# Pooling mixer: moving sums on VectorE, means by constants, dt's small steps in other banks, wide norms by Ln and Exp

## The chip, the core and the metric

The kernel runs on one core of a Trainium2 chip. The metric is the device time of one launch in microseconds (us). Of the core's engines five matter: TensorE (PE in the rows; PEld is its weight load), VectorE (DVE), ScalarE (ACT), GpSimd (POOL) and SyncE (SP), which issues most of the DMA transfers. Each engine works through its own instructions in the order in which they stand, and waits on semaphores for the others. TensorE's clock has two levels, 1.2 and 2.4 GHz; the rows give the granted one as a share of 2.4 GHz (PEclk).

## What is computed

Two layers of a backbone over 512 latent tokens and 256 context tokens. In a layer one wide projection feeds a bidirectional state-space mixer (conv, dt, scan) and a pooling mixer; the two are merged by gates, and a SwiGLU sub-layer follows. The modulation vectors (adaLN) come from a small product of a condition with large weights. The last layer needs no pooling of the context.

```python
# sizes: D_MODEL 1024, SEQ 512 (8 rows of 64), CTX_LEN 256, DEPTH 2, POOL_WIDTH 1024
POOL_WINDOWS = (2, 4, 8, 16)

def rmsnorm(x, g):
    xf = x.astype(jnp.float32)
    y = xf * lax.rsqrt(jnp.mean(xf * xf, axis=-1, keepdims=True) + EPS)
    return (y * g).astype(x.dtype)

def pool_minus_self(u):
    L = u.shape[-2]
    ...
    for gi, k in enumerate(POOL_WINDOWS):
        lo = jnp.clip(t - k // 2, 0, L)
        hi = jnp.clip(t + k // 2, 0, L)
        seg = cs[..., gi * POOL_GROUP:(gi + 1) * POOL_GROUP]
        s = jnp.take(seg, hi, axis=-2) - jnp.take(seg, lo, axis=-2)
        outs.append(s / (hi - lo).astype(jnp.float32)[:, None])
    mean = jnp.concatenate(outs, axis=-1)
    return (mean - uf).astype(u.dtype)

# a layer, for latent and context alike
h = modulate(rmsnorm(x, g_mix[l]), sh1, sc1)
proj = h @ w_in            # z, xbc (conv, then SSD), dt, u_pool, gate logits
dt = softplus(dt_raw + dt_bias)
pm = pool_minus_self(u_pool)          # latent: along each row of 64; context: along 256
pm = einsum('blgi,gio->blgo', pm by 4 groups, pool_w)
o_pool = (pm * pool_scale) @ w_pool_out
x = x + ga1 * ((g_ssd * o_ssd + g_pool * o_pool) @ w_out)
x = x + ga2 * swiglu(modulate(rmsnorm(x, g_ffn[l]), sh2, sc2), ...)
```

## The kernel before

Activations stand as 128 channels on the partitions by tokens in the free dimension: 768 columns in layer 0 (512 latent, 256 context), 512 in layer 1's pooling. A matmul in f32 is done as three in fp32r (lines 199 to 201): operands are split in a high part (a cast on ScalarE, whi at L176 for weights, L524 for activations) and a low part (a subtraction on VectorE, wlo at L178, L525). An *item* is one 128-row tile of a product; `K.run` issues items one after the other, and their results go to eight PSUM banks in rotation: pl (2), ptr (2), pc, pst, and py (2), where py is not in the items' rotation. Weights are fetched by SyncE into three raw buffers (L173).

`pool_path` is the part of a layer in which pooling is done. It runs, in this order:

- eight u items, the pooling input. ScalarE copies each result into one of two padded tiles pu, in which a row of 64 tokens has eight zeros on both sides. Then `fin` makes the moving sum: VectorE adds neighbours (L568), GpSimd adds shifted sums for windows 4, 8 and 16 (L573, none to three adds, twelve a layer), VectorE multiplies by rc, a table of 1/count (L576, context L580), subtracts pu (L578, L581) and the result pm is split (L524, L525) into pq.
- the dt item, evicted by ScalarE to dtraw (L625).
- eight pw items (the grouped product, two pooled tiles each; evicted at L600 and split) and eight po items (the output product, evicted at L611). A pw item asks for two of the pooled tiles; the last two items ask for the eighth.

Beside the items run *side generators*, one step each whenever matmuls worth 2150 ns have been issued (`K.tick`). `dt_gen` turns dtraw into decay factors: transposes (copied by VectorE at L658), a chain of small VectorE operations (L660 to L671, with a polynomial at L666), cumulative sums by matmuls (L679 to L689), and rows written back to memory (L708 transposes, L711 the low part sw on VectorE, then DMAs of arow, erow and jrow; Ln at L731). `ada_vec` makes modulation vectors: it loads 128x512 pieces of adaLN weights into tiles aw and multiplies and sums each on VectorE (L396): 64 products of 32 pieces in layer 0, 32 of 32 in layer 1. `K.drain` ends both before the conv part begins.

`Rms.fin` ends a norm: a matmul with ones sums the squares, then for wide norms (1024 channels) ScalarE's Sqrt (L440) and VectorE's reciprocal (L442), for narrow ones (256) Ln and Exp on ScalarE.

The order of instructions on each engine is made by a tile scheduler that simulates engines; `high_priority` moves an instruction ahead, and `issue_after` keeps it behind a named one.

Of the kernel before, what the change touches and what calls it, by code (L numbers as in the profile page):

```python
# [9 lines left out]
F32 = mybir.dt.float32  # L10
# [6 lines left out]
P = 128  # L17
# [271 lines left out]
def tile_hybrid_ssd_pool_dit(ctx, tc, xin, cond, condr, wada, wadt, pk, win, wdt, wso, wpw, wpo, wo, wgu, wdn,  # L289
# [78 lines left out]

    def ada_vec(l, secs, pool, tag, bufs, stile, burst=1):

# [13 lines left out]
        for i, (h, s, k) in enumerate(todo):  # L384
            if (s, k) == (secs[0], 0):
                sb = [stile() for _ in range(nj)]
                for j in range(nj):
                    nc.sync.dma_start(sb[j], srow[j:j + 1, h * 512:(h + 1) * 512].to_broadcast([P, 512]))
            if i + 1 < len(todo):
                load()  # L390
            for j in range(nj):
                if done % burst == 0:
                    yield
                done += 1
                o = ws[i] if j == nj - 1 else K.tile(pool, tag, bufs, [P, 512])
                V.scalar_tensor_tensor(o[:], ws[i][:], 1.0, sb[j], op0=ALU.mult, op1=ALU.mult,  # L396
                                       accum_out=acc[:, secs.index(s), h, k, j:j + 1])
            if h == 1 and k == KT - 1:
                m = mods[l][:, s]
                V.tensor_tensor(m[:, :, :nj], acc[:, secs.index(s), 0], acc[:, secs.index(s), 1], op=ALU.add)  # L400
                ada_fin(l, s, m, [m[:, q::2, :nj] for q in range(2)], nj)

    class Rms:
# [6 lines left out]
        def add(self, t):  # L410
            c0, c1 = self.c0, self.c1
            q = K.tile(self.pool, "tmp" if self.w == CW else "u", self.tb, [P, self.w])
            A.activation(q[:, c0:c1], t[:, self.off + c0:self.off + c1], AF.Square)
            self.q = q
            if self.acc is None:
                self.acc = q
            else:
                self.eng.tensor_tensor(self.acc[:, c0:c1], self.acc[:, c0:c1], q[:, c0:c1], op=ALU.add)

        def fin(self, m):  # L420
# [3 lines left out]
            if m == 1024:  # L424
                warm = K.tile(cst, "warm", 1, [P, 1])
                A.activation(warm[:], self.q[:, c0:c0 + 1], AF.Sqrt)
            eps = epst if m == 1024 else epsg
            for a in range(c0, c1, 512):
# [4 lines left out]
                else:  # L433
# [5 lines left out]
                    T.matmul(o, oner[:], al, start=False, stop=True)  # L439
                A.activation(r[:, a:b], o, AF.Sqrt if m == 1024 else AF.Ln, bias=eps[:], scale=1.0 / m)  # L440
            if m == 1024:
                V.reciprocal(r[:, c0:c1], r[:, c0:c1])  # L442
            else:
                A.activation(r[:, c0:c1], r[:, c0:c1], AF.Exp, scale=-0.5)

# [77 lines left out]
    def split(t, hi, lo, n):  # L523
        A.copy(hi[:, :n], t[:, :n])  # L524
        V.tensor_tensor(lo[:, :n], t[:, :n], hi[:, :n].bitcast(F32), op=ALU.subtract)  # L525

    def pool_path(l, acts, cx, dp, first, nxt, secs):
# [3 lines left out]
        with K.pool(f"pu{l}", 1) as pup, K.pool(f"pp{l}", 2) as pp, K.pool(f"px{l}", 1) as px:  # L531
# [13 lines left out]
            def u_item(i, r, w=None):  # L545
# [12 lines left out]
                def fin():  # L558
# [7 lines left out]
                    with tc.high_priority() if i < HOT else nullcontext():  # L566
# [3 lines left out]
                        for st in range(1, gi + 1):  # L570
                            sh = 1 << st
                            ln -= sh
                            G.tensor_tensor(s[:, :ln], s[:, :ln], s[:, sh:sh + ln], op=ALU.add)  # L573
                        o = 8 - (1 << gi)
                        r3 = lambda t: t[:, :LAT].rearrange("p (r w) -> p r w", w=64)
                        V.tensor_tensor(r3(pm), s[:, :640].rearrange("p (r w) -> p r w", w=80)[:, :, o:o + 64], r3(rc),  # L576
                                        op=ALU.mult)
                        V.tensor_tensor(r3(pm), r3(pm), ul[:, :, 8:72], op=ALU.subtract)  # L578
                        if cx:
                            V.tensor_tensor(pm[:, LAT:], s[:, 640 + o:640 + o + CTX], rc[:, LAT:], op=ALU.mult)  # L580
                            V.tensor_tensor(pm[:, LAT:], pm[:, LAT:], u[:, 648:904], op=ALU.subtract)  # L581
                        split(pm, *pms[i], n)

# [65 lines left out]
    def dt_gen(l, D, dp):  # L649
# [37 lines left out]
        suf = K.psum("ptr")
        T.matmul(suf[:, :192], mk[:, M_GT:M_GT + P], daf[:, :192], start=True, stop=True)
# [735 lines left out]
```

## Time and profile before

| | us |
|---|---|
| median of 3 runs (2915.68 to 2917.33) | 2916.78 |
| the profiled execution | 2918.18 |
| its span in the profile | 2916.4 |
| busy: TensorE | 2809.3 (96%) |
| busy: VectorE | 2047.1 (70%) |
| busy: ScalarE | 1289.1 (44%) |
| busy: GpSimd | 754.2 (26%) |

Times in the profile are counted from the start of the span. A window shows how long each engine was busy in a stretch; a waits view shows for how long an engine stood in front of an instruction and whose signal ended that; a timeline lists instructions with start, duration and, in brackets, the idle time before them with its releaser. Pooling lies at about 55 to 200 us (layer 0) and 1709 to 1815 us (layer 1).

### The profile page before, as it was taken

What the parts mean: (1) busy time and instruction counts of PE and PEld (TensorE: products, weight loads), DVE (VectorE), ACT (ScalarE), POOL (GpSimd) and SP (SyncE); (2) the same over time, 40 slices, a digit from 0 to 9 for tenths busy, and PEclk for the clock granted to TensorE, in tenths of its full rate; (3) what the DMA queues carried; (4) which work ended last, traced back from release to release, by engine and by line L of the source; (5) the groups of instructions that cost most, each with busy time, mean ns of one, the idle gap of its engine ahead of it and who ended that gap; (6) DMA issues with size and microseconds to landing.
All of it is one profiled execution on the core that took longest, in us unless ns stands there. A gap on an engine that the chain in (4) does not pass through costs nothing.

```text
span 2916.4 us, 43006 instructions
## 1 busy us (share of the span) xinstructions
PE 2809.3 (96%) x16384; PEld 2467.8 (85%) x16384; DVE 2047.1 (70%) x3231; ACT 1289.1 (44%) x2102; POOL 754.2 (26%) x695
## 2 busy tenths in 40 slices
PE   6899999999999999999999988999999989999998
PEld 4688888888889998899999976878888868889998
DVE  6965677777754678856666696677777746877776
ACT  4244544555544124333333454455455542545443
POOL 1300323322221112222222132032322211334443
PEclk8999999999999999999999999999999999999999
DMA  7362222222236754312222365322332248523333
GB/s 262 124 174 86 72 83 90 80 76 80 79 94 203 260 184 134 117 58 78 68 66 73 92 195 151 102 84 94 95 98 87 99 158 310 163 85 98 98 102 119
DMA packets 172847, 347.79 MB, mean 119 GB/s; under 512 B 33312, under 2 KB 74048, under 8 KB 172640
## 3 DMA queue, kind: packets, MB, share of 16 engines
q1 hardware_dynamic: 151872, 314.79, 33.8%
q0 software_dynamic: 12448, 13.20, 1.9%
q10 hardware_dynamic: 8320, 17.05, 1.6%
q8 instruction: 129, 2.11, 0.3%
q14 instruction: 78, 0.64, 0.1%
HBM read 310.20 MB, written 34.74 MB: 118 GB/s over the span
## 4 chain that ended last, share of the span: by engine, by line
PE 83%; DVE 7%; issue 3%; DMA 3%; ACT 2%; POOL 1%; SPq 0%; DVEq 0%; ACTq 0%; POOLq 0%
PE pl L201 11%; PE pl L200 11%; PE pl L199 10%; PE pc L199 4%; PE pc L200 4%; PE pc L201 4%; PE ptr L200 3%; PE ptr L199 3%; PE ptr L201 3%; PE pl L261 3%; PE pl L262 3%; PE pl L263 3%; PE pst L789 2%; PE py L860 2%; PE py L831 2%
## 5 line engine op out<-in xcount | busy, mean ns | idle before, releaser
L199 PE MATMUL pl<-h,whi 128*128 128x512 f32 (+2 forms) x1481 | 565.4, 382 | 6.4 <-ACT whi L176 2.8
L201 PE MATMUL pl<-h,whi 128*128 128x512 f32 (+2 forms) x1481 | 561.9, 379 | 1.8 <-DVE h L466 1.8
L200 PE MATMUL pl<-h,wlo 128*128 128x512 f32 (+2 forms) x1481 | 559.1, 378 | 2.1 <-DVE wlo L178 2.0
L176 ACT CAST whi<-raw 128x1024 fp32r<-128x1024 f32 (+5 forms) x340 | 314.2, 928 | 545.9 <-PE pl L201 167.9
L178 DVE TENSOR_TENSOR wlo<-raw,whi 128x1024 fp32r<-128x1024 f32 (+5 forms) x328 | 374.4, 1144 | 176.4 <-ACT whi L176 168.8
L199 PEld LDWEIGHTS pl<-h,whi 128*128 128x128 f32 x1481 | 279.5, 189 | 55.7 <-issue 8.3
L201 PEld LDWEIGHTS pl<-h,whi 128*128 128x128 f32 x1481 | 279.1, 188 | 52.5 <-issue 7.3
L200 PEld LDWEIGHTS pl<-h,wlo 128*128 128x128 f32 x1481 | 279.4, 189 | 49.9 <-issue 7.3
L199 PE MATMUL pc<-h,whi 128*128 128x256 f32 (+2 forms) x923 | 283.8, 307 | 15.1 <-ACT h L524 12.8
L201 PE MATMUL pc<-h,whi 128*128 128x256 f32 (+2 forms) x923 | 284.1, 308 | 1.7 <-DVE h L459 1.6
L200 PE MATMUL pc<-h,wlo 128*128 128x256 f32 (+2 forms) x923 | 280.0, 303 | 3.1 <-DVE wlo L178 3.1
L1013 DVE SCALAR_TENSOR_TENSOR cv<-up,pk,cv 128x770 f32<-128x770 f32 (+1 forms) x256 | 258.8, 1012 | 21.8 <-ACT cv L1011 15.9
L780 POOL TENSOR_TENSOR sct<-cs,dec 128x256 f32<-128x256 f32 x128 | 125.1, 982 | 441.8 <-ACT cs L791 270.3
L199 PEld LDWEIGHTS pc<-h,whi 128*128 128x128 f32 x923 | 176.3, 191 | 30.0 <-ACT h L524 13.3
L200 PEld LDWEIGHTS pc<-h,wlo 128*128 128x128 f32 x923 | 176.5, 191 | 13.3 <-DVE wlo L178 3.5
L201 PEld LDWEIGHTS pc<-h,whi 128*128 128x128 f32 x923 | 176.3, 191 | 11.9 <-issue 3.8
L200 PE MATMUL ptr<-h,wlo 128*128 128x384 f32 (+3 forms) x493 | 170.4, 346 | 2.9 <-DVE wlo L178 2.8
L199 PE MATMUL ptr<-h,whi 128*128 128x384 f32 (+3 forms) x493 | 170.5, 346 | 1.3 <-ACT whi L176 1.1
L201 PE MATMUL ptr<-h,whi 128*128 128x384 f32 (+3 forms) x493 | 169.4, 344 | 0.0
L863 POOL TENSOR_TENSOR y<-y,ea 128x512 f32<-128x512 f32 x64 | 91.0, 1422 | 243.5 <-DVE ea L862 231.8
L117 POOL TENSOR_TENSOR ss<-raw 128x512 f32<-128x512 f32 x37 | 54.3, 1467 | 342.6 <-DMA raw<-in_wgu 269.7
L105 DVE TENSOR_TENSOR wlo<-raw,whi 128x1024 fp32r<-128x1024 f32 x74 | 111.2, 1502 | 16.4 <-ACT whi L104 16.2
(358 smaller groups left out, 6695.3 us busy)
## 6 DMA issues: line engine op xcount, KB each, us to landing
raw<-in_win SPq DMA_DIRECT2D x144, 512.0 KB, 3.4
raw<-in_wgu SPq DMA_DIRECT2D x92, 512.0 KB, 3.3
aw<-in_wadt SPq DMA_DIRECT2D x64, 256.0 KB, 3.7
ea<-erow SPq DMA_DIRECT2D x128, 128.0 KB, 3.1
raw<-in_wso SPq DMA_DIRECT2D x32, 512.0 KB, 4.7
ss<-in_wadt SPq DMA_DIRECT2D x64, 256.0 KB, 4.0
raw<-in_wo SPq DMA_DIRECT2D x26, 512.0 KB, 3.7
raw<-in_wdn SPq DMA_DIRECT2D x48, 192.0 KB, 2.4
```

Source lines behind the costliest of these rows:

```text
L105: k.nc.vector.tensor_tensor(l, t, h.bitcast(F32), op=ALU.subtract)
L176: nc.scalar.copy(hi[:, :n], raw[:, :n])
L178: e.tensor_tensor(lo[:, :n], raw[:, :n], hi[:, :n].bitcast(F32), op=ALU.subtract)
L199: T.matmul(o, wh, ah[:, c0:c1], start=first, stop=False)
L200: T.matmul(o, wl, ah[:, c0:c1], start=False, stop=False)
L201: T.matmul(o, wh, al[:, c0:c1], start=False, stop=last)
L261: nc.tensor.matmul(o, wh[:, m], ah, start=bool(first) and k == 0, stop=False, skip_group_check=True)
L262: nc.tensor.matmul(o, wl[:, m], ah, start=False, stop=False, skip_group_check=True)
L263: nc.tensor.matmul(o, wh[:, m], al, start=False, stop=k == len(acts) - 1, skip_group_check=True)
L780: G.tensor_tensor(t[:].rearrange("p (h q) -> p h q", h=4), cs[src][:, d, :].rearrange("p (h q) -> p h q", h=4), D["dec"][:, d, c, h0:h0 + ...
L863: G.tensor_tensor(y[pr][:, :LAT], y[pr][:, :LAT], ea[:, :LAT], op=ALU.add)
L1013: V.scalar_tensor_tensor(t[:, :e], u[:, i:i + e], cw(i), t[:, :e], op0=ALU.mult, op1=ALU.add)
```

## The change

1. The further adds of the moving sums go from GpSimd to VectorE (L581 of the new program).
2. The mean is taken with a constant, 1 / window, fused with the subtraction (L590); the first and last eight columns of each row, where the true count may be smaller, are then written again with rc (L591, L592).
3. The adaLN products of `pool_path` are kept behind the split of the last pooled tile (`issue_after`).
4. Each step of `dt_gen` gets high priority, and its PSUM tiles are from the py banks.
5. Wide norms take Ln and Exp, both in one activation table, which is loaded explicitly behind the last square; Sqrt and the reciprocal go. The table loads that stood ahead of dt's Exp and Ln (L662, L713, L731) are no longer in the program.

```diff
     # ada_vec(..., after=None)
-                V.scalar_tensor_tensor(o[:], ws[i][:], 1.0, sb[j], op0=ALU.mult, op1=ALU.mult,
-                                       accum_out=acc[:, secs.index(s), h, k, j:j + 1])
+                with tc.issue_after(after) if after else nullcontext():
+                    V.scalar_tensor_tensor(o[:], ws[i][:], 1.0, sb[j], op0=ALU.mult, op1=ALU.mult,
+                                           accum_out=acc[:, secs.index(s), h, k, j:j + 1])
...
             if m == 1024:
                 warm = K.tile(cst, "warm", 1, [P, 1])
-                A.activation(warm[:], self.q[:, c0:c0 + 1], AF.Sqrt)
+                with tc.issue_after(self.last):
+                    load = A.preload_act_table_set("natural_log_exp_and_others")
+                with tc.issue_after(load.ins):
+                    A.activation(warm[:], self.q[:, c0:c0 + 1], AF.Ln, bias=epst[:])
...
-                A.activation(r[:, a:b], o, AF.Sqrt if m == 1024 else AF.Ln, bias=eps[:], scale=1.0 / m)
-            if m == 1024:
-                V.reciprocal(r[:, c0:c1], r[:, c0:c1])
-            else:
-                A.activation(r[:, c0:c1], r[:, c0:c1], AF.Exp, scale=-0.5)
+                A.activation(r[:, a:b], o, AF.Ln, bias=eps[:], scale=1.0 / m)
+            A.activation(r[:, c0:c1], r[:, c0:c1], AF.Exp, scale=-0.5)
...
+    def urgent(gen):
+        while True:
+            with tc.high_priority():
+                if next(gen, StopIteration) is StopIteration:
+                    return
+            yield
...
-                            G.tensor_tensor(s[:, :ln], s[:, :ln], s[:, sh:sh + ln], op=ALU.add)
+                            V.tensor_tensor(s[:, :ln], s[:, :ln], s[:, sh:sh + ln], op=ALU.add)
...
-                        V.tensor_tensor(r3(pm), s[:, :640].rearrange("p (r w) -> p r w", w=80)[:, :, o:o + 64], r3(rc),
-                                        op=ALU.mult)
-                        V.tensor_tensor(r3(pm), r3(pm), ul[:, :, 8:72], op=ALU.subtract)
+                        parts = [(s[:, :640].rearrange("p (r w) -> p r w", w=80)[:, :, o:o + 64], ul[:, :, 8:72],
+                                  r3(pm), r3(rc), lambda t: t.rearrange("p r (e w) -> p r e w", w=8)[:, :, 0:8:7, :])]
...
+                        for sv, uv, pv, rv, ends in parts:
+                            V.scalar_tensor_tensor(pv, sv, 0.5 / (1 << gi), uv, op0=ALU.mult, op1=ALU.subtract)
+                            V.tensor_tensor(ends(pv), ends(sv), ends(rv), op=ALU.mult)
+                            V.tensor_tensor(ends(pv), ends(pv), ends(uv), op=ALU.subtract)
+                        D["last"] = split(pm, *pms[i], n)
...
-            K.side.append(dt_gen(l, D, dp))
-            K.side.append(ada_vec(l, secs, pp, "aw", 3 if cx else 4, lambda: K.tile(pp, "asb", 2 if cx else 4, [P, 512])[:], 2))
+            K.side.append(urgent(dt_gen(l, D, dp)))
+            K.side.append(ada_vec(l, secs, pp, "aw", 3 if cx else 4, lambda: K.tile(pp, "asb", 2 if cx else 4, [P, 512])[:], 2, D["last"]))
...
     # dt_gen: five such lines (the others: cum, tot, suf and rows())
-        t = K.psum("ptr")
+        t = K.psum("py")
```

On VectorE, layer 0, around the last of the eight pooled tiles: sw is the moving sum, pm the pooled tile, pu the padded input, aw an adaLN product. Before, these are successive rows:

```order
L568 TENSOR_TENSOR sw_978<-pu_415 128x911
L396 SCALAR_TENSOR_TENSOR aw_1491,acc_1067<-aw_1491,asb_1071 128x512
L576 TENSOR_TENSOR pm_913<-sw_912,rc_910 128x512
L580 TENSOR_TENSOR pm_913<-sw_912,rc_910 128x256
L178 TENSOR_TENSOR wlo_1057<-raw_1054,whi_1056 128x1024
L396 SCALAR_TENSOR_TENSOR aw_1548,acc_1067<-aw_1508,asb_1070 128x512
L578 TENSOR_TENSOR pm_913<-pm_913,pu_410 128x512
L581 TENSOR_TENSOR pm_913<-pm_913,pu_410 128x256
L396 SCALAR_TENSOR_TENSOR aw_1508,acc_1067<-aw_1508,asb_1071 128x512
L396 SCALAR_TENSOR_TENSOR aw_1575,acc_1067<-aw_1528,asb_1070 128x512
L525 TENSOR_TENSOR pq_915<-pm_913,pq_914 128x768
```

The seventh tile's means stand behind the eighth's first add there, with four adaLN products between. Now:

```order
L576 TENSOR_TENSOR sw_994<-pu_417 128x911
L178 TENSOR_TENSOR wlo_1075<-raw_1072,whi_1074 128x1024
L581 TENSOR_TENSOR sw_994<-sw_994 128x909
L526 TENSOR_TENSOR pq_929<-pm_927,pq_928 128x768
L581 TENSOR_TENSOR sw_994<-sw_994 128x905
L581 TENSOR_TENSOR sw_994<-sw_994 128x897
L590 SCALAR_TENSOR_TENSOR pm_995<-sw_994,pu_417 128x512
L590 SCALAR_TENSOR_TENSOR pm_995<-sw_994,pu_417 128x256
L591 TENSOR_TENSOR pm_995<-sw_994,rc_924 128x8x2x8
L591 TENSOR_TENSOR pm_995<-sw_994,rc_924 128x2x8
L592 TENSOR_TENSOR pm_995<-pm_995,pu_417 128x8x2x8
L592 TENSOR_TENSOR pm_995<-pm_995,pu_417 128x2x8
```

The three further adds stand in VectorE's queue, the mean is two operations with four small ones behind, and no adaLN product is among them.

On ScalarE, layer 0, around the eviction of dt's item (dtraw). Before:

```order
L625 ACTIVATE dtraw_1020<-ptr_992,pk_82 64x512
L524 CAST pq_914<-pm_913 128x768
L176 CAST whi_1296<-raw_1294 128x1024
L625 ACTIVATE dtraw_1020<-pl_1022,pk_82 64x256
L600 ACTIVATE pm_1078<-pc_1060,pk_82 128x512
```

And now:

```order
L636 ACTIVATE dtraw_1038<-ptr_1010,pk_82 64x512
L176 CAST whi_1314<-raw_1312 128x1024
L636 ACTIVATE dtraw_1038<-pl_1040,pk_82 64x256
L525 CAST pq_996<-pm_995 128x768
L611 ACTIVATE pm_1096<-pc_1078,pk_82 128x512
```

The cast of a pooled tile stood between the two halves of dtraw and now stands behind both; before it was the seventh tile's, now it is the eighth's.

On VectorE, layer 1, the stretch around dt's first copy (dtv). Before:

```order
L396 SCALAR_TENSOR_TENSOR aw_16777,acc_16309<-aw_16777,asb_16573 128x512
L396 SCALAR_TENSOR_TENSOR aw_16780,acc_16309<-aw_16780,asb_16573 128x512
L658 COPY dtv_16368<-ptr_16361 128x384
L178 TENSOR_TENSOR wlo_16476<-raw_16473,whi_16475 128x1024
L400 TENSOR_TENSOR mod_85<-acc_16309 128x8
L660 TENSOR_SCALAR dte_16370<-dtv_16368 128x384
L576 TENSOR_TENSOR pm_16188<-sw_16187,rc_16185 128x512
```

And now:

```order
L526 TENSOR_TENSOR pq_16257<-pm_16255,pq_16256 128x512
L397 SCALAR_TENSOR_TENSOR aw_16340,acc_16339<-aw_16340,asb_16342 128x512
L397 SCALAR_TENSOR_TENSOR aw_16344,acc_16339<-aw_16344,asb_16342 128x512
L397 SCALAR_TENSOR_TENSOR aw_16363,acc_16339<-aw_16363,asb_16342 128x512
L397 SCALAR_TENSOR_TENSOR aw_16366,acc_16339<-aw_16366,asb_16342 128x512
L526 TENSOR_TENSOR pq_16350<-pm_16351,pq_16349 128x512
L526 TENSOR_TENSOR pq_16369<-pm_16370,pq_16368 128x512
L397 SCALAR_TENSOR_TENSOR aw_16419,acc_16339<-aw_16419,asb_16342 128x512
L669 COPY dtv_16398<-py_16391 128x384
L397 SCALAR_TENSOR_TENSOR aw_16422,acc_16339<-aw_16422,asb_16342 128x512
L178 TENSOR_TENSOR wlo_16506<-raw_16503,whi_16505 128x1024
```

Before, the last adaLN products stand ahead of dtv and means of pooled tiles behind it; now the pooled tiles are all split (the first row is the last of them) and the first products follow, with the splits of pw.

## Rows read from the trace of the kernel before

**Rows 1.** Windows: start:end length, busy us (count) PE, PEld, DVE, ACT, POOL, PEclk, DMA, GB/s

```profile
62.00:120.00 58.00, 58.00 (x335) 49.94 (x335) 57.81 (x86) 18.31 (x28) 19.43 (x9) 1.00 0.41 132
119.80:135.50 15.70, 5.74 (x32) 4.62 (x30) 15.60 (x25) 2.12 (x3) 6.41 (x6) 0.81 0.30 102
135.50:147.00 11.50, 8.48 (x30) 6.88 (x31) 9.29 (x21) 6.67 (x12) 1.97 (x6) 0.67 0.73 223
178.00:200.00 22.00, 17.67 (x100) 15.01 (x99) 8.05 (x19) 8.85 (x15) 0.00 (x0) 0.92 0.59 136
1664.00:1709.00 45.00, 36.54 (x194) 33.08 (x193) 41.01 (x77) 33.20 (x82) 15.12 (x20) 0.85 0.46 145
1709.00:1752.00 43.00, 41.95 (x196) 33.61 (x196) 42.88 (x78) 13.06 (x19) 9.64 (x6) 1.00 0.74 237
1752.00:1769.00 17.00, 7.60 (x34) 5.24 (x32) 17.00 (x27) 5.76 (x8) 10.78 (x6) 0.87 0.50 163
1769.00:1779.00 10.00, 7.11 (x18) 5.14 (x19) 9.93 (x23) 5.48 (x10) 1.98 (x9) 0.54 0.40 117
38.00:62.00 24.00, 21.83 (x101) 16.91 (x102) 18.53 (x28) 16.74 (x33) 8.53 (x17) 0.87 0.51 166
```

**Rows 2.** Waits of TensorE, 119 to 200 us: us, times, longest

```profile
PE pl L199 <- ACT dtraw L625: 10.0, 1, 10.0
PE ptr L199 <- DVE dtv L658: 2.9, 1, 2.9
```

**Rows 3.** Waits of TensorE, 1709 to 1790 us

```profile
PE ptr L199 <- DVE dtv L658: 8.2, 1, 8.2
```

**Rows 4.** Timeline of ScalarE, layer 0: start, us, instruction, idle before it

```profile
133.38 0.83 ACT L524 CAST pq<-pm 128x768 fp32r<-128x768 f32 x1 [15.14 <-DVE pm L581]
```

**Rows 5.** Timelines of VectorE in both pooling stretches

```profile
72.46 1.10 DVE L568 TENSOR_TENSOR sw<-pu 128x911 f32<-128x911 f32 x1
...
73.81 2.19 DVE L396 SCALAR_TENSOR_TENSOR aw<-aw,asb 128x512 f32<-128x512 f32 x1
...
77.07 0.68 DVE L396 SCALAR_TENSOR_TENSOR aw<-aw,asb 128x512 f32<-128x512 f32 x1
...
143.24 0.95 DVE L525 TENSOR_TENSOR pq<-pm,pq 128x768 fp32r<-128x768 f32 x1
...
171.06 0.17 DVE L400 TENSOR_TENSOR mod<-acc 128x16 f32<-128x16 f32 x1
...
1709.13 0.82 DVE L568 TENSOR_TENSOR sw<-pu 128x639 f32<-128x639 f32 x1
...
1775.62 0.68 DVE L525 TENSOR_TENSOR pq<-pm,pq 128x512 fp32r<-128x512 f32 x1
```

**Rows 6.** Timeline of ScalarE at layer 1's first norm and at the last norm

```profile
1667.06 1.28 ACT L426 ACT_TABLE_LOAD   x1
1668.35 0.20 ACT L426 ACTIVATE warm<-u 128x1 f32<-128x1 f32 x1
...
2906.39 0.47 ACT L440 ACTIVATE rr<-py,epst 128x256 f32<-128x256 f32 x1 [1.01 <-PE py L432]
```

**Rows 7.** All reciprocals of line 442 after the kernel's start: min, median, max ns

```profile
L442 DVE RECIPROCAL rr<-rr x8: 1743/2153/2553, 1110.3 to 2906.9; 128x384 f32<-128x384 f32 x4, 128x256 f32<-128x256 f32 x4
```

**Rows 8.** Costliest groups of the page: busy us, mean ns, idle before

```profile
L178 DVE TENSOR_TENSOR wlo<-raw,whi 128x1024 fp32r<-128x1024 f32 (+5 forms) x328 | 374.4, 1144 | 176.4 <-ACT whi L176 168.8
```

**Rows 9.** Timeline of GpSimd, an add of layer 0's pooling

```profile
73.63 1.82 POOL L573 TENSOR_TENSOR sw<-sw 128x909 f32<-128x909 f32 x1 [17.39 <-DVE sw L568]
```

**Rows 10.** DMA issues of the page: KB each, us to landing

```profile
aw<-in_wadt SPq DMA_DIRECT2D x64, 256.0 KB, 3.7
```

**Rows 11.** Waits of VectorE, 119 to 210 us

```profile
DVE sw L711 <- DMA arow<-sw: 6.9, 1, 6.9
DVE aw L396 <- DMA aw<-in_wadt: 5.1, 3, 4.3
```

**Rows 12.** Groups of VectorE by form, 1709 to 1752 us: busy us, mean ns, idle before

```profile
L396 DVE SCALAR_TENSOR_TENSOR aw<-aw,asb 128x512 f32<-128x512 f32 x24 | 18.7, 811 | 0.0
```

More of the change, by code (lines that the diff above doesn't have):

```diff
@@ L367, in ada_gen, with ada_vec @@
             yield
-    def ada_vec(l, secs, pool, tag, bufs, stile, burst=1):
+    def ada_vec(l, secs, pool, tag, bufs, stile, burst=1, after=None):
         nj = 2 if l == 0 else 1
@@ L412, in add @@
             q = K.tile(self.pool, "tmp" if self.w == CW else "u", self.tb, [P, self.w])
-            A.activation(q[:, c0:c1], t[:, self.off + c0:self.off + c1], AF.Square)
+            self.last = A.activation(q[:, c0:c1], t[:, self.off + c0:self.off + c1], AF.Square).ins
             self.q = q
@@ L524, in split @@
         A.copy(hi[:, :n], t[:, :n])
-        V.tensor_tensor(lo[:, :n], t[:, :n], hi[:, :n].bitcast(F32), op=ALU.subtract)
+        return V.tensor_tensor(lo[:, :n], t[:, :n], hi[:, :n].bitcast(F32), op=ALU.subtract).ins
+    def urgent(gen):
[4 more added lines that the diff above has]
+            yield
     def pool_path(l, acts, cx, dp, first, nxt, secs):
@@ L572, in fin @@
                             ln -= sh
-                            G.tensor_tensor(s[:, :ln], s[:, :ln], s[:, sh:sh + ln], op=ALU.add)
+                            V.tensor_tensor(s[:, :ln], s[:, :ln], s[:, sh:sh + ln], op=ALU.add)
                         o = 8 - (1 << gi)
                         r3 = lambda t: t[:, :LAT].rearrange("p (r w) -> p r w", w=64)
-                        V.tensor_tensor(r3(pm), s[:, :640].rearrange("p (r w) -> p r w", w=80)[:, :, o:o + 64], r3(rc),
-                                        op=ALU.mult)
-                        V.tensor_tensor(r3(pm), r3(pm), ul[:, :, 8:72], op=ALU.subtract)
+                        parts = [(s[:, :640].rearrange("p (r w) -> p r w", w=80)[:, :, o:o + 64], ul[:, :, 8:72],
+                                  r3(pm), r3(rc), lambda t: t.rearrange("p r (e w) -> p r e w", w=8)[:, :, 0:8:7, :])]
                         if cx:
-                            V.tensor_tensor(pm[:, LAT:], s[:, 640 + o:640 + o + CTX], rc[:, LAT:], op=ALU.mult)
-                            V.tensor_tensor(pm[:, LAT:], pm[:, LAT:], u[:, 648:904], op=ALU.subtract)
-                        split(pm, *pms[i], n)
+                            parts.append((s[:, 640 + o:640 + o + CTX], u[:, 648:904], pm[:, LAT:], rc[:, LAT:],
+                                          lambda t: t.rearrange("p (e w) -> p e w", w=8)[:, 0:32:31, :]))
+                        for sv, uv, pv, rv, ends in parts:
[3 more added lines that the diff above has]
+                        D["last"] = split(pm, *pms[i], n)
                 return dict(w=w or K.W(win[l, 48 + i]), acts=acts, rg=r, ev=ev)
@@ L677, in dt_gen @@
         daf = v[:]
-        cum = K.psum("ptr")
+        cum = K.psum("py")
         T.matmul(cum[:, :192], mk[:, M_LE:M_LE + P], daf[:, :192], start=True, stop=True)
@@ L682, in dt_gen @@
                cum[:, :384].rearrange("p (d c h) -> p c d h", d=2, c=6))
-        tot = K.psum("pst")
+        tot = K.psum("py")
         T.matmul(tot[:, :384], mk[:, M_ONE:M_ONE + P], daf, start=True, stop=True)
@@ L686, in dt_gen @@
         A.activation(dec[:].rearrange("p d c h -> p (d c h)"), tot[:, :384], AF.Exp)
-        suf = K.psum("ptr")
+        suf = K.psum("py")
         T.matmul(suf[:, :192], mk[:, M_GT:M_GT + P], daf[:, :192], start=True, stop=True)
@@ L705, in rows @@
             for o, n in ((0, 4), (4, 2)):
-                t = K.psum("ptr")
+                t = K.psum("py")
                 for c in range(n):
```

## The prediction, made before the changed kernel ran

> **What bounds the kernel now.** I read the windows first, to see where TensorE is not at full work [rows 1], then the waits of TensorE [rows 2, 3], then the timelines of the engine each wait names. TensorE is busy for most of the span, so a change pays only where it idles or runs at the low granted clock. The change touches four such places.
>
> *Layer 0 behind the pooling items.* In the stretch 62 to 120 us TensorE is without a gap and at clock 1.00, but VectorE is busy 57.81 of 58.00 us [rows 1]: it is behind. From 119.80 to 135.50 TensorE works 5.74 of 15.70 us, from 135.50 to 147 8.48 of 11.50, from 178 to 200 17.67 of 22.00. The waits are one of 10.0 us for ScalarE's dtraw, then 2.9 for VectorE's dtv [rows 2]. ScalarE is not slow there: it stood 15.14 us in front of a cast of pm, waiting for VectorE's L581 [rows 4], and dtraw is queued behind that cast. The last pooled tile is split on VectorE only at 143.24 [rows 5], 23 us after TensorE wanted to begin pw. *Layer 1* has the same: 9.4 us idle in 1752 to 1769, 2.9 in 1769 to 1779, the largest wait 8.2 us for VectorE's dtv [rows 1, 3].
>
> After each idle stretch the granted clock is at 1.2 GHz for a while: 0.67 over 135.5 to 147, 0.54 over 1769 to 1779. A mean of 0.67 means two thirds of the time at half speed; busy time spent there costs half of itself.
>
> Loss, layer 0: 9.96 idle; 3.02 idle + half of 0.66 x 8.48 = 5.8; 4.33 idle + half of 0.16 x 17.67 = 5.7. **Sum 21.5 us.** Layer 1: 9.40 + half of 0.26 x 7.60 = 10.4; 2.89 + half of 0.92 x 7.11 = 6.2. **Sum 16.6 us.**
>
> *Front of layer 1*, 1664 to 1709: 8.46 idle + half of 0.30 x 36.54 = **13.9 us** lost, VectorE 41.01 of 45 busy. *Start*, 38 to 62: 2.2 idle + half of 0.26 x 21.83 = 5.0. *End*: after the last norm's ScalarE step of 0.47 us VectorE's reciprocal of 256 columns takes 1.75 alone [rows 6, 7].
>
> **Part 1 and 2: sums to VectorE, mean by a constant.** VectorE gets 12 more adds a layer. An add of two 128x911 operands takes it 1.10 us [rows 5]. A pooled tile then costs VectorE: first add 1.1; 1.1 for each further one (0 to 3); the two fused multiply-subtracts of 768 columns about 1.1 (0.95 for one operation of 768, [rows 5]); four corrections of at most 256 elements a partition, 0.17 each by a small operation [rows 5], 0.7; split 0.95; the weights' wlo 1.14 [rows 8]. That is 5.0 + 1.1 x further adds; over eight tiles 40 + 13 = 53 us. TensorE needs 8.3 us an item (335 matmuls in 58.00 us, 48 an item), 67 for eight. So VectorE, now always behind, keeps up, once the 33 adaLN products that stand between the tiles are gone.
>
> The sums on VectorE also remove a second cost: while POOL adds (1.82 us from 73.63, [rows 9]), VectorE's product that started at 73.81 takes 2.19 us instead of 0.68 [rows 5]. SBUF — State Buffer of the Trainium skill, section Who interferes with whom, has a rule for it: an operation of VectorE with two SBUF inputs and a reading GpSimd shut each other out for a whole instruction; the row agrees. Its page Perfetto Trace Analysis, section Optimizing Scalar/DVE Operations, speaks against the change: with VectorE saturated, work may go to GpSimd, though it adds that the shared port can undo that; by the first half the 13 us of adds would come out of the gain, near rival C's time; by the rows just named the holding cost more than a saved add.
>
> TensorE ends the eighth pooling item 8.3 us (the dt item) ahead of 119.8, at 111.5. VectorE then has the last tile's 8.3 us: last split at about **120 instead of 143**. pw asks for that tile only in its seventh item, about 11.5 us in. So the wait of 10.0 is gone, and dtraw no longer stands behind a cast (ScalarE's order, in the part on the change). In layer 1 a tile costs about 3.7 + 0.86 x further adds (0.82 for an add of 639 columns, and the work between), 40 us for eight, begun at 1709 as now and with 2 us of other work between: last split at **1751 instead of 1775.6** [rows 5], needed about 1759.
>
> **Part 3: products held to the last split.** They do not vanish. In layer 0, 64 products of 0.68 (44 us) now lie behind 120, with eight splits, ten wlo and dt's steps, some 70 us: done at 191, while conv's first steps follow at 200 and TensorE meets each wlo 15 us or more after VectorE. That is covered. In layer 1, 24 products and seven splits stand ahead of the wlo of the fourth po item: 24 x 0.68 + 7 x 0.6 + 3 x 1.14 + dt's small steps 3 = 27 us, so 1778, and TensorE wants it at about 1780. The cover is 2 us if loads keep up. They are 20 x 256 KB [rows 10] plus some 2 MB of weights in 27 us, about 265 GB/s; the stretch 1709 to 1752 moved 237 at a DMA share of 0.74 [rows 1], so the limit is near 320. I take **3 us** lost there, bounds 0 and 10.
>
> **Part 4: dt urgent, in py banks.** dt's first copy now comes with the early dtraw, so the 2.9 and 8.2 us of [rows 2, 3] end. Its pst and ptr banks no longer hold up pw and po. What may stay: VectorE writes sw for lj only when arow's 16 transfers have read it; it waited 6.9 us for that [rows 11]. TensorE's last transposes run in layer 0 during po, in layer 1 at conv's start. I take **2.5 us** lost in layer 0 and **2 us** in layer 1, bounds 0 and 8 each.
>
> Pooling together: layer 0 21.5 - 2.5 = 19.0, layer 1 16.6 - 5 = 11.6.
>
> **Part 5: Ln and Exp for wide norms.** Eight reciprocals of 1.74 to 2.55 us [rows 7], and the kernel start's, leave VectorE; ScalarE gets an Exp for each, which I price as the step of 0.47 for 256 columns [rows 6], and a table load of 1.28 [rows 6] in front of every wide norm, also where none stood; it lies under the sums of squares and their matmul, as the one at 1667.06 does. In the front of layer 1 two reciprocals of 2.55 stand on a saturated VectorE: 5.1 gone, 1.2 added on the chain; I take **4.5** (0 to 10, the loss is 13.9). Start, with the price of a 256-column reciprocal, 1.75 - 0.5 = **1.3**; channel sub-layer's norm in layer 1 **0.7** (0 to 3); end 1.75 - 0.47 = 1.28, less 0.2 for a load that ends late, **1.1**. ScalarE's next step came 1.29 us after the load's start [rows 6], so it costs its 1.28 and no more. ScalarE: Activation LUTs of the Trainium skill, What ACT_TABLE_LOAD costs, adds about 1.38 us of drain to 1.28; no such gap stands in the row, and by the page the end's 1.1 would be about -0.3.
>
> **Sum:** 19.0 + 11.6 + 4.5 + 1.3 + 0.7 + 1.1 = 38.2. The profiled execution took 2918.18, 1.4 above the median; 2916.78 - 38.2 = **2878.6**, forecast **2878**.
>
> **Rivals.**
> A, *dt or the products come late* (VectorE's queue in order, wlo behind products that wait for loads): TensorE stops at the upper bounds in two of the three places, some 5.5 + 6 us more: **2890**. For: a cover of 2 us in layer 1; the 6.9 us row. Against: 15 us of cover in layer 0.
> B, *norms give nothing*: front, start, sub-layer and end are paced by the squares and splits; minus 7.6: **2886**. For: ScalarE, 33.20 of 45 busy at 1664, gets load and Exp.
> C, *it does not do what it says*: TensorE is released by pooling, but pw goes no faster than ScalarE's evictions and VectorE's splits of pw (1.7 us an item against 1.9), and half of both pooling terms returns as waits on ScalarE: **2894**.
> D, *slower: adaLN's loads pace VectorE*. One load lands in 3.7 us [rows 10]; if loads came one at a time with a product of 0.68 behind each, 4.4 us a load, layer 1's wlo behind 24 products (20 loads after the first four) comes at 1751 + 88 = 1839, 59 us late; layer 0's last of 32 at 121 + 29 x 4.4 = 249 against 225, 24 late. 83 - 38 = 45 slower: **2962**. It decides from the pace at which the lateness eats 38 us: 20p - 29 = 38, p = 3.4 us a load. Against: 24 products in the 43 us of 1709 to 1752 have 0.0 us idle before them [rows 12], under 1.8 us each with VectorE never waiting; over the 91 us after 119 all waits for loads sum to 5.1 [rows 11].
>
> **Chances.** Forecast 0.60 (2863 to 2886), A 0.17, B 0.08, C 0.06, D 0.09 (of it 0.04 at a pace near 3.4, too near before's time to be told apart). 0.2%, 5.8 us, is about what a measurement can tell from no change. Faster 0.90, of which C's worst end gives 0.01 to same; same 0.05, slower 0.05. The low end is the bounds that favour the change: 2916.8 - 21.5 - 16.6 - 10 - 1.3 - 3 - 1.1 = 2863. The high end, 2898, takes in A, B and C.
>
> **What would show it.** After: the last pooling split near 120 and 1751; no wait for dtraw after 119; the granted clock 1.00 from 62 to 175; a product of 512 columns never above 0.7 us in the pooling. Waits for aw over 1 us or for wlo in 1775 to 1800 would speak for A or D; VectorE still saturated in 1664 to 1709 with TensorE idle as before for B; waits for pm in pw for C. I am wrong if TensorE's idle time around 120 to 147 and 1752 to 1779 only moves to 150 to 200 and 1780 to 1820.

## The result

The changed kernel takes 2882.74 us (2881.90 to 2885.02) against 2917.06 of the kernel before in the same comparison: 34.3 us less, ratio 0.988 with a 95% interval of 0.9868 to 0.9891. The forecast was 2878, the range 2863 to 2898. The profiled execution of the changed kernel has a span of 2881.2 us; everything behind the places in question stands some 20 us earlier in layer 1's beginning, so stretches of after are shifted against [rows 1].

The windows of the changed kernel (length; busy us and count of PE, PEld, DVE, ACT, POOL; PEclk; DMA share; GB/s):

```profile
62.00:120.00 58.00, 58.00 (x340) 49.84 (x339) 47.92 (x83) 20.30 (x32) 2.13 (x9) 1.00 0.25 84
119.80:135.50 15.70, 15.70 (x90) 13.51 (x89) 15.04 (x33) 13.80 (x22) 0.00 (x0) 1.00 0.57 176
147.00:175.00 28.00, 28.00 (x166) 24.69 (x165) 17.25 (x43) 9.59 (x20) 0.00 (x0) 1.00 0.67 204
195.00:240.00 45.00, 39.83 (x216) 33.96 (x215) 32.15 (x71) 11.61 (x17) 1.21 (x2) 0.96 0.63 179
1642.00:1687.00 45.00, 37.73 (x212) 34.48 (x210) 38.25 (x79) 37.55 (x88) 14.78 (x20) 0.92 0.49 152
1731.00:1757.00 26.00, 26.00 (x114) 20.73 (x112) 21.90 (x56) 11.89 (x20) 0.00 (x0) 1.00 0.75 242
1757.00:1772.00 15.00, 8.81 (x30) 6.62 (x30) 13.12 (x33) 4.70 (x7) 0.00 (x0) 0.77 0.95 312
```

VectorE fell from 57.81 to 47.92 us in 62 to 120, TensorE went from 5.74 to 15.70 busy in 119.8 to 135.5, and its clock stays at 1.00 through 175 us. The stalls of [rows 2, 3] are gone. But two new holes stand where conv begins in layer 0 (5.2 us idle in 195 to 240) and at the fourth po item of layer 1 (6.2 idle in 1757 to 1772, at 0.77 of the clock). What is queued there shows in a timeline of VectorE, and in TensorE's row at the second hole:

```profile
118.88 0.95 DVE L526 TENSOR_TENSOR pq<-pm,pq 128x768 fp32r<-128x768 f32 x1
...
179.47 1.01 DVE L722 TENSOR_TENSOR sw<-py,sw 64x512 fp32r<-64x512 f32 x2 [12.76 <-DMA arow<-sw]
...
189.71 0.69 DVE L397 SCALAR_TENSOR_TENSOR aw<-aw,asb 128x512 f32<-128x512 f32 x1 [2.95 <-DMA aw<-in_wadt]
...
193.76 0.69 DVE L397 SCALAR_TENSOR_TENSOR aw<-aw,asb 128x512 f32<-128x512 f32 x1 [2.61 <-DMA aw<-in_wadt]
...
197.88 0.69 DVE L397 SCALAR_TENSOR_TENSOR aw<-aw,asb 128x512 f32<-128x512 f32 x1 [1.67 <-DMA aw<-in_wadt]
...
201.29 0.69 DVE L397 SCALAR_TENSOR_TENSOR aw<-aw,asb 128x512 f32<-128x512 f32 x1 [1.98 <-DMA aw<-in_wadt]
...
204.49 0.69 DVE L397 SCALAR_TENSOR_TENSOR aw<-aw,asb 128x512 f32<-128x512 f32 x1 [1.77 <-DMA aw<-in_wadt]
...
1730.72 0.69 DVE L526 TENSOR_TENSOR pq<-pm,pq 128x512 fp32r<-128x512 f32 x1
...
1762.97 1.22 DVE L178 TENSOR_TENSOR wlo<-raw,whi 128x1024 fp32r<-128x1024 f32 x1
```

```profile
1764.24 0.79 PE L200 MATMUL pl<-pq,wlo 128*128 128x512 f32 x1 [4.58 <-DVE wlo L178]
```

The last pooled tile is split at 118.88 instead of 143.24 [rows 5], and in layer 1 at 1730.72. The adaLN products that were held back for this now wait for their loads on a VectorE that works in order, and weights' wlo stand behind them. The waits of VectorE over 119 to 240 us say how much, and the one below them is TensorE's for wlo in the same stretch:

```profile
DVE aw L397 <- DMA aw<-in_wadt: 18.8, 11, 3.4
DVE sw L722 <- DMA arow<-sw: 12.8, 1, 12.8
PE pl L200 <- DVE wlo L178: 4.3, 3, 3.1
```

Before, VectorE's two waits were 5.1 and 6.9 us, over 119 to 210 [rows 11].

By place, idle time plus half of the busy time at 1.2 GHz, in the two traces:

| place | before | after | saved | forecast |
|---|---|---|---|---|
| start, to the pooling | | | 3.4 (the same matmul starts at 56.7, then 53.3) | 1.3 |
| pooling of layer 0 to early conv | 22.9 | 6.8 | 16.1 | 19.0 |
| front of layer 1 | 14.3 | 10.7 | 3.6 | 4.5 |
| pooling of layer 1 to early conv | 17.6 | 9.5 | 8.1 | 11.6 |
| channel norm, layer 1 | 8.9 | 4.6 | 4.3 | 0.7 |
| end | 11.6 | 10.4 | 1.1 | 1.1 |

They sum to 36.6; the spans differ by 35.2, because the changed kernel also loses a little between these places.

### The profile page after: what moved, and what is told of

Its sections match the earlier page's. It is cut to its first block, busy times and chain, and to the rows that moved or that the text cites. A ratio compares the mean times of both kernels' runs of the same rounds, so it can differ in the third digit from the quotient of the medians.

```text
span 2881.2 us, 43014 instructions
## 1 busy us (share of the span) xinstructions
PE 2798.9 (97%) x16384; PEld 2460.0 (85%) x16384; DVE 2016.0 (70%) x3269; ACT 1289.2 (45%) x2109; POOL 713.2 (25%) x671
## 4 chain that ended last, share of the span: by engine, by line
PE 84%; DVE 5%; DMA 5%; issue 3%; ACT 2%; POOL 1%; SPq 1%; DVEq 0%; ACTq 0%; POOLq 0%
PE pl L200 10%; PE pl L201 10%; PE pl L199 10%; PE pc L199 4%; PE pc L201 4%; PE pc L200 4%; PE ptr L200 3%; PE ptr L201 3%; PE ptr L199 3%; PE pl L261 3%; PE pl L262 3%; PE pl L263 3%; PE pst L800 2%; PE py L871 2%; PE py L842 2%
## 5 line engine op out<-in xcount | busy, mean ns | idle before, releaser
L178 DVE TENSOR_TENSOR wlo<-raw,whi 128x1024 fp32r<-128x1024 f32 (+5 forms) x328 | 367.1, 1122 | 122.8 <-ACT whi L176 122.0
L200 PEld LDWEIGHTS pl<-h,wlo 128*128 128x128 f32 x1481 | 279.1, 188 | 58.3 <-DVE wlo L178 11.3
L1024 DVE SCALAR_TENSOR_TENSOR cv<-up,pk,cv 128x770 f32<-128x770 f32 (+1 forms) x256 | 258.6, 1013 | 22.9 <-ACT cv L1022 17.4
L199 PEld LDWEIGHTS pc<-h,whi 128*128 128x128 f32 x923 | 176.1, 191 | 29.3 <-ACT h L525 13.4
L117 POOL TENSOR_TENSOR ss<-raw 128x512 f32<-128x512 f32 x37 | 53.3, 1439 | 346.5 <-DMA raw<-in_wgu 329.2
```

What stands on the lines that cost most here:

```text
L178: e.tensor_tensor(lo[:, :n], raw[:, :n], hi[:, :n].bitcast(F32), op=ALU.subtract)
L199: T.matmul(o, wh, ah[:, c0:c1], start=first, stop=False)
L200: T.matmul(o, wl, ah[:, c0:c1], start=False, stop=False)
L1024: V.scalar_tensor_tensor(t[:, :e], u[:, i:i + e], cw(i), t[:, :e], op0=ALU.mult, op1=ALU.add)
```

## Experiments

Each undoes or mends something in the changed kernel. *Saved* is always the median of before minus that of the kernel, before having run in the same comparison (2918.63, 2916.68 and 2916.54 in the three). The changed kernel saves 34.3. By the recorded 95% intervals its saving is good to 3.4 us either way, those of the other kernels to 4 to 6, so a difference of two savings under some 6 us is not shown by the times alone. *Aligned by matmul* means that the n-th matmul of one trace is set against the n-th of the other.

**The hold undone.**

```diff
-...lambda: K.tile(pp, "asb", ...)[:], 2, D["last"]))
+...lambda: K.tile(pp, "asb", ...)[:], 2))
```

> The changed kernel with part 3 undone: the adaLN products of the pooling path may stand anywhere again. Theory (the hold is what lets VectorE keep up): some 33 products of 0.69 us, 23 us, come back between the pooled tiles of layer 0, which fill VectorE already, so its last split comes near 140 instead of 119, TensorE waits about 12 us in pw, and layer 1 likewise by half of that; the 12 us now lost at the beginning of conv (6.8 in layer 0, 7.5 behind 1760 in layer 1) shrink to some 4. Time near 2895. Rival (the hold only shifts the products, and their lateness is the change's own loss): near 2873, faster than the changed kernel.

2890.86, saved 27.8: the hold is worth 6.5, just clear of noise. Both mechanisms are there. In 62 to 122 us VectorE is busy 57.75 of 60 again, with 24 products between the pooled tiles, and pw waits in layer 1 for VectorE through ScalarE's pm and pq:

```profile
L397 DVE SCALAR_TENSOR_TENSOR aw<-aw,asb 128x512 f32<-128x512 f32 x24 | 16.4, 684 | 0.0
```

```profile
PE pc L199 <- ACT pm L611: 7.7, 1, 7.7
PE ptr L199 <- ACT pq L525: 3.3, 1, 3.3
```

(First the group of products in 62 to 122 us, then TensorE's waits in 1700 to 1830.) On the other side nothing is lost at either start of conv: idle 0.0 in 175 to 245 and 1760 to 1830. Aligned by matmul, this trace is 5.8 us behind the changed one at 192 us and 2.0 ahead at 252; in layer 1 it goes from 1.4 ahead at 1731 to 18.0 behind at 1755 and is 4.3 behind at 1830. So most of what the hold gains in the pooling it gives back a little later, and what is left of it comes from layer 1. In layer 0 the theory expected too much: the last pooled tile is done at 127 us and not near 140, and TensorE waits 3.5 us in pw and not 12.

**The sums on GpSimd again.**

```diff
-                            V.tensor_tensor(s[:, :ln], s[:, :ln], s[:, sh:sh + ln], op=ALU.add)
+                            G.tensor_tensor(s[:, :ln], s[:, :ln], s[:, sh:sh + ln], op=ALU.add)
```

> The changed kernel with part 1 undone: the further adds of the moving sums on GpSimd again, all else as changed. Theory (an add on GpSimd holds VectorE's two-operand work for as long as it lasts, so nothing is saved by moving it): the last split of layer 0 comes within 3 us of 119 or later, operations of VectorE beside the adds last 2 us or more again, time 2880 to 2890. Rival (VectorE is full, so work off it helps): 13 us of adds less on VectorE, time near 2878 or below.

2889.32, saved 29.3: part 1 is worth 5.0, too little for the times alone to show. The rival's 2878 is out. In 62 to 122 us VectorE is busy only 42.38 us, yet stands 10.4 us in front of its means, and an operation with two operands that meets an add is longer (an add of GpSimd and two splits of VectorE from the timelines; then groups of VectorE by form, this kernel and the changed one):

```profile
69.37 2.62 POOL L581 TENSOR_TENSOR sw<-sw 128x909 f32<-128x909 f32 x1 [17.05 <-DVE sw L576]
70.34 2.46 DVE L526 TENSOR_TENSOR pq<-pm,pq 128x768 fp32r<-128x768 f32 x1
75.26 0.96 DVE L526 TENSOR_TENSOR pq<-pm,pq 128x768 fp32r<-128x768 f32 x1 [0.90 <-ACT pq L525]
```

```profile
L526 DVE TENSOR_TENSOR pq<-pm,pq 128x768 fp32r<-128x768 f32 x7 | 9.7, 1385 | 4.7 <-ACT pq L525 4.7
L590 DVE SCALAR_TENSOR_TENSOR pm<-sw,pu 128x512 f32<-128x512 f32 x8 | 5.5, 687 | 10.4 <-POOL sw L581 10.4
L591 DVE TENSOR_TENSOR pm<-sw,rc 128x16 f32<-128x16 f32 x7 | 2.7, 379 | 0.0
```

```profile
L526 DVE TENSOR_TENSOR pq<-pm,pq 128x768 fp32r<-128x768 f32 x9 | 8.6, 957 | 5.3 <-ACT pq L525 5.3
L591 DVE TENSOR_TENSOR pm<-sw,rc 128x16 f32<-128x16 f32 x8 | 1.4, 169 | 0.0
```

The means mix two kinds: of the seven splits, five take 0.96 us as in the changed kernel, and the two that meet an add 2.45 and 2.46; of the seven products of 16 elements, six take 0.16 to 0.17 us and one 1.66. In layer 0, idle time and low clock cost 11.8 us here and 6.8 in the changed kernel: the adds on GpSimd lose though VectorE then has time to spare.

**Both undone.**

> The changed kernel with parts 1 and 3 both undone: sums on GpSimd and the adaLN products free, that is, nearly the pooling of the kernel before, with dt's and the norms' parts as changed. Alone, part 1 was worth 6.5 us and part 3 8. Theory (each covers for the other: with either one undone VectorE still keeps up after a fashion, with both it is full again and the adds hold its products): more than the sum of 14.5, some 18 to 24 us slower, 2900 to 2907. Rival (they add up): 2897.

2900.71, saved 15.8: together the two are worth 18.5, more than 6.5 + 5.0 (the 8 and 6.5 expected above compare the times and not the savings), but the excess of 7.0 comes from four savings with 3 to 5 us either way each, so the times alone don't show it. The traces do, for layer 0: the second half of dtraw is evicted at 117.6 us in the changed kernel, at 118.0 with the hold undone, at 120.3 with the sums undone, and at 132.3 with both undone (135.1 before). Aligned at 252 us, the kernel is 2.0 ahead of the changed one without the hold, 4.8 behind with sums on GpSimd, and 9.9 behind with both. So there each covers in part for the other. TensorE's waits in layer 0, with pw and dt behind a late VectorE again as in [rows 2]:

```profile
PE py L667 <- ACT dtraw L636: 10.9, 1, 10.9
PE pl L199 <- ACT pm L611: 2.0, 1, 2.0
```

**dt without priority, in the old banks.**

```diff
-            K.side.append(urgent(dt_gen(l, D, dp)))
+            K.side.append(dt_gen(l, D, dp))
-        t = K.psum("py")            # and the others of dt_gen
+        t = K.psum("ptr")           # tot: "pst"
```

> The changed kernel with part 4 undone: dt's steps without priority and in the ptr and pst banks. Theory (dt's banks and its place were a third of the stalls before, 2.9 and 8.2 us, but with dtraw and the pooled tiles early they would be short anyway): 2 to 8 us slower, near 2888. Rival (the early dtraw alone did it, and dt's urgency only pulls its long chain of small steps and 32 row transfers ahead of the adaLN products and loads): same or faster, 2878 to 2883.

2899.05, saved 19.6: part 4 is worth 14.7, the largest of the five by the medians, nearly all in layer 1. Theory and rival both missed it. It is not that dt's chain on VectorE is late: its last step (L682) starts at 1773.01 here and at 1773.81 in the changed kernel. TensorE reaches the products of it too early:

```profile
1773.62 1.01 PE L690 MATMUL ptr<-dtv,mk 128*128 128x192 f32 x2 [7.59 <-DVE dtv L682]
```

To tell the banks from the priority, each was undone alone.

> The changed kernel with only the banks of part 4 undone: dt's steps keep their priority, their PSUM tiles come from ptr and pst again. With all of part 4 undone the time was 2899, 16 us above the changed kernel, most of it in layer 1. Theory (the banks do it: in ptr and pst dt's matmuls stand in the queue between items and hold their banks while they wait for VectorE): most of the 16 us come back, 2892 to 2899. Rival (the priority does it, since VectorE's chain for dt is late otherwise): within 4 us of the changed kernel.

> The changed kernel with only the priority of part 4 undone: dt's PSUM tiles stay in py, its steps have no priority. Theory (the banks do it): within 5 us of the changed kernel, 2880 to 2888. Rival (the priority does it): TensorE waits for dt's products (7.6 us in front of the cumulative sums with all of part 4 undone) and the time is 2892 or more.

With priority in the old banks 2905.44, saved 11.1, 23 us short of the changed kernel; without priority in py 2879.37, saved 37.2, the same as the changed kernel within its interval. The banks do it all, and in the old banks the priority even costs 8.5, most of it in layer 0 (the first wait below). TensorE's waits with priority in the old banks, 100 to 250 us and then 1690 to 1840:

```profile
PE ptr L199 <- DVE sw L722: 6.7, 1, 6.7
```

```profile
PE ptr L690 <- DVE dtv L682: 5.8, 1, 5.8
PE pl L201 <- DVE pq L526: 4.7, 3, 2.7
```

The order of TensorE in layer 1 tells why. In ptr and pst, dt's products stand ahead of the po items that take the same banks after them in the program, the item in pst among them; only two items, both in pl, stand ahead of them:

```
L201 MATMUL pl_16746<-pq_16492,whi_16579 128x512
L690 MATMUL ptr_16552<-dtv_16398,mk 128x192
L691 MATMUL ptr_16552<-dtv_16398,mk 128x192
L695 MATMUL pst_16556<-dtv_16398,mk 128x384
...
L199 MATMUL pst_16589<-pq_16349,whi_16505 128x512
```

In py they stand 83 rows further back (an item of po is 24 rows), in the middle of the sixth item, and that item in pst is done before them:

```
L200 MATMUL ptr_16843<-pq_16427,wlo_16671 128x512
L690 MATMUL py_16552<-dtv_16398,mk 128x192
L691 MATMUL py_16552<-dtv_16398,mk 128x192
L695 MATMUL py_16556<-dtv_16398,mk 128x384
L201 MATMUL ptr_16843<-pq_16428,whi_16670 128x512
```

**Wide norms by Sqrt and reciprocal again.**

> The changed kernel with part 5 undone: wide norms by Sqrt and reciprocal again. Theory (the differences by place between the two traces are what the norms give): start 3.4, front of layer 1 about 3, layer 1's channel norm 2.5, end 0.6 come back, so near 2892, and the rest of the trace as changed. Rival (the gain at these places has another origin, such as the order the scheduler happened to make): within 3 us of the changed kernel.

2895.61, saved 23.0: part 5 is worth 11.3. Aligned by matmul, this trace falls behind the changed one by 3.4 us at the start, 3.6 in the front of layer 1, 3.2 between 2463 and 2567 and 1.1 at the end, 11.3 at the norms' own places. It also loses 3.1 in layer 0 behind 192, 1.7 behind 1060 and 1.5 near 2835, and makes up 1.6 in layer 1's pooling. The 1.7 and 1.5 stand at dips of the granted clock to 0.5; the one near 2835 is also in the kernel with part 4 undone, which has Ln and Exp, so it can't be put down to the norms. The undoing brings back dt's three table loads a layer too (130.9, 168.2 and 170.2 us in layer 0), which the prediction gave no price; whether the 3.1 are theirs or the scatter of DMA waits is open. At the end, ScalarE before (its last square, then Sqrt), and in the changed kernel:

```profile
2904.73 0.42 ACT L413 ACTIVATE u<-x 128x256 f32<-128x256 f32 x1 [2.10 <-DVE x L1172]
...
2906.39 0.47 ACT L440 ACTIVATE rr<-py,epst 128x256 f32<-128x256 f32 x1 [1.01 <-PE py L432]
```

```profile
2870.71 0.42 ACT L414 ACTIVATE u<-x 128x256 f32<-128x256 f32 x1 [2.10 <-DVE x L1183]
2871.14 1.28 ACT L428 ACT_TABLE_LOAD   x1
2872.44 0.30 ACT L430 ACTIVATE warm<-u,epst 128x1 f32<-128x1 f32 x1
2872.64 0.46 ACT L444 ACTIVATE rr<-py,epst 128x256 f32<-128x256 f32 x1
2873.12 0.42 ACT L445 ACTIVATE rr<-rr 128x256 f32<-128x256 f32 x1
```

Ln starts 1.5 us after the end of the last square where Sqrt had started after 1.24, and Exp takes 0.42 in place of the reciprocal's 1.75.

**The mean by the table again** (two products and two subtractions for every tile).

> The changed kernel with part 2 undone: every mean is a product with the table of counts and a subtraction, so a tile of layer 0 has four operations (0.68, 0.41 twice) instead of two fused ones and four small ones. Theory (it is even: 2.0 us against 1.03 + 0.75): within 2 us of the changed kernel, 2881 to 2885. Rival (VectorE sets pooling's end, every microsecond of a tile counts eight times): 0.2 to 0.4 us a tile later or 3 us in each layer, near 2886.

2882.78, saved 33.9: part 2 is worth nothing that can be measured; with the hold, VectorE has time in the pooling (47.92 of 58.00).

**What sets the new hole in layer 0.** First, own tiles for dt's last rows, so that they wait for no transfer:

```diff
-        rows(lj, hl[0], hl[1], False)
+        hl = [K.tile(D["pup"], "pm", 2, [P, W])[:64, :W].bitcast(F32R) for _ in range(2)]
+        rows(lj, hl[0], hl[1], False)
```

> The changed kernel with two more tiles for dt's last rows (lj), so that VectorE writes them without waiting for the arow transfers (12.8 us in layer 0, 8.2 in layer 1). Theory (this wait puts the adaLN products behind it late, and these put conv's first wlo late): layer 0's wait for wlo of 4.3 us behind 200 goes, time 2876 to 2879. Rival (the pace of the adaLN loads, 3.3 us each, sets the end; they wait for a tile, not for VectorE): within 1.5 us of the changed kernel.

2883.90, saved 32.8: no gain. The wait for arow is gone, but VectorE then waits for loads (10.5) and their broadcast operand (7.5) in 160 to 240, and TensorE still 5.9 for wlo. Second, a place for the unread product:

```diff
-                o = ws[i] if j == nj - 1 else K.tile(pool, tag, bufs, [P, 512])
+                o = ws[i] if j == nj - 1 else junk if junk is not None else K.tile(pool, tag, bufs, [P, 512])
```

> The changed kernel, but the elementwise result of the first of two products on a piece, which nobody reads, goes to a pooling tile that is free by then, instead of taking one of the three tiles of the adaLN loads. Theory (with two tiles a piece only about one load is under way, hence 3.3 us a load): waits of VectorE for these loads fall from 18.8 us to under 6, conv's first wlo is on time, time 2876 to 2879. Rival (the wait for arow of 12.8 us alone makes them late): within 1.5 us of the changed kernel, the loads only wait elsewhere.

2873.93, saved 42.8, 8.5 more than the changed kernel. One of its four runs took 2884.57, the others 2872.24 to 2874.63; the second kernel with this mend, below, confirms the gain. VectorE's waits in 119 to 240 us:

```profile
DVE sw L722 <- DMA arow<-sw: 10.5, 1, 10.5
DVE wlo L178 <- ACT whi L176: 9.5, 5, 5.8
DVE pu L397 <- DMA aw<-in_wadt: 4.8, 5, 1.3
```

The arow wait is nearly as long as it was, the loads' wait fell from 18.8 to 4.8, and TensorE has no idle time in 175 to 245. So the pace of the loads was the cause of the hole in layer 0, and the cause of that pace was that a piece took two of three tiles.

**The new hole in layer 1.**

```diff
-ada_vec(..., 3 if cx else 4, ...)
+ada_vec(..., 3 if cx else 8, ...)
```

> The changed kernel with eight instead of four tiles for the adaLN loads in layer 1. Theory (the 4.6 us in front of the fourth po item are the 5.6 us that VectorE waits for loads between the last split and that wlo): the waits for loads behind 1731 fall under 1.5 us, the stall of 4.6 and the low clock behind it go, time 2875 to 2877. Rival (24 products of 0.69 us in front of that wlo are too many by themselves): a stall of 2 us or more stays at 1760, time near 2881.

> The changed kernel with two mends: the unread result of the first of two products on a piece goes to a free pooling tile (layer 0; 9 us faster alone), and eight tiles for the adaLN loads in layer 1 (1.6 us faster alone, with the stall of 4.6 us gone). Theory (they mend two places apart): 2870 to 2873. Rival (layer 1's mend is worth nothing, its stall moves): 2874.

Eight tiles alone: 2881.11, saved 35.6; with the mend of layer 0: 2874.39, saved 42.2. In both the stall of 4.6 us is gone and VectorE waits for no load behind 1731, as the theory has it, but the times don't move beyond their scatter: of 9.5 us lost behind 1731 the last kernel still loses 5.2, now in small waits for pq, for ScalarE's up and whi. So the number of tiles sets the wait for wlo there, but its size is not steady: in the kernel with the mend of layer 0 alone, whose layer 1 is that of the changed kernel, it is 2.0 us and the loss behind 1731 7.0. A gain from mending it is not shown. The two kernels with the mend of layer 0 are the fastest measured, ratio 0.9856 (0.9836 to 0.9877 alone, 0.9842 to 0.9871 with eight tiles).

## Why the prediction was right, and where its steps were off

*What bounds the kernel* held: TensorE lost its time where it was said to, and VectorE's queue was the reason. The signs named beforehand came: last splits at 118.88 (forecast 120) and at 1730.72, 44 us after layer 1's first add (forecast 42, from 1709 to 1751); clock 1.00 from 62 to 175; no wait for dtraw; no product held. Rival C did not come: TensorE is busy all through pw. But the sign named for A and D came too, with waits for aw up to 3.4 us and the 4.6 for wlo, and part of the idle time did move to where conv begins.

*Parts 1 to 3.* The tile's price held: VectorE was busy 47.92 us of 58.00 in the pooling, a share of 0.83, where 53 of 67 or 0.79 had been forecast. The reason held in part. The prediction gave sums and hold one price together and took both to be needed; in layer 0 either one alone frees dtraw by 120.3 us, both undone cost 18.5. The losses of the kernel before were 22.9 and 17.6 us and not 21.5 and 16.6: the sums left out the low clock in 119.80 to 135.50 and the idle time behind 1779.

*The failed step is the cover in layer 0.* I let 64 products follow at VectorE's own pace and found 15 us of room. The step that broke it is that I took the products at 0.68 us each: behind 189 us they came at the pace of their loads, 3.2 to 4.1 us a piece (the waits above stand 3.7 apart on the mean up to 204.49), after a wait for arow that had grown from 6.9 to 12.8 us but whose removal alone gained nothing. The row I set against rival D, no idle time before 24 products, was from a stretch in which loads had pooled tiles to hide behind, and from layer 1, where a piece takes one tile; layer 0's piece takes two of three, which the code says and I did not count. Loss 6.8 instead of 2.5. In layer 1 the cover of 2 us was too thin: its wlo started 32 us after the last split where it was to be done after 27, with 5.6 us of waits for loads between; I took 5 us of loss in all and 9.5 were lost (7.0 in the trace with the mend of layer 0, whose layer 1 is the same). So most of rival A came true, 8.8 us more loss for its 11.5, by a mechanism that is also D's: loads that pace VectorE, though only for part of the products.

*Part 4* was priced as the end of the old waits, by the early dtraw; that ptr and pst no longer hold up pw and po was named and given no price of its own. The runs show that in layer 1 the banks decide: in the old ones layer 1 loses 23 us where before had lost 17.6, though dtraw is early, since TensorE meets dt's products three and a half po items too soon. That term was inside the sum as the absence of the old waits, so the total did not suffer; the explanation did. In py the priority has no measurable effect.

*Part 5* was undersized: 7.6 forecast, 11.3 measured. The front of layer 1 and the end were near (4.5 and 1.1 against 3.6 and 1.1); the start (3.4 for 1.3) and layer 1's channel norm (3.2 to 4.3 for 0.7) gave more. I took these from the reciprocal's length alone; what else stands behind them was not tested. Rival B is dead. The table load cost its 1.28 us and the next step followed at once (1.30 us after its start), as in [rows 6]. The drain that ScalarE: Activation LUTs of the Trainium skill (What ACT_TABLE_LOAD costs) adds is not in these rows.

By the table of places, pooling gave 24.2 us for a forecast of 30.6 and the norms 12.4 for 7.6. That the forecast's 38.2 came within 4 us of 34.3 is in part luck: errors of both signs met. The parts measured by undoing (18.5 for parts 1 and 3, 14.7, 11.3 and nothing for part 2) sum to 44.5, more than 34.3: each is priced in a kernel that has the others, and they are not a sum.

## What to carry to other kernels

Work that is held back to free an engine comes back at the pace of its slowest supply: count the buffers that one step of it really takes, and follow what is queued behind it on the in-order engine. A small side chain should not share PSUM banks with a rotation of large items: here the sharing fixed its place in TensorE's queue, and priority did not mend that (11.1 saved with it, 19.6 without). And undo parts alone and in pairs; two parts that cover for each other look small one at a time.

## What was not expected of the hardware

An add of GpSimd holds VectorE's small operations as long as its large ones: one product of 16 elements a partition that met an add took 1.66 us, six others 0.16 to 0.17. Whether GpSimd is held in turn is not shown: its adds of 909 columns took 1.71 to 2.62 us with the sums on GpSimd again and 1.82 to 2.56 in the kernel before. Behind 1757 us, with the held loads and the weights together, the DMA engines ran at a share of 0.95 with 312 GB/s, which fits the prediction's estimate of a limit near 320; the kernel before has 0.89 with 310 over 2406 to 2479 us.
